# Block 2's gate in seven half-size products, with two of four weight sums made by accumulating DMAs

## The chip, the cores and the metric

One NeuronCore of a Trainium2 chip runs the whole kernel in one launch. The metric is the device time in microseconds (us); the median of three runs of the kernel before is 755.2 us. The engines spoken of are TensorE (PE, with its weight loads PEld), VectorE (DVE), ScalarE (ACT), GpSimd (POOL) and SyncE (SP), whose queue issues all DMAs of the kernel before.

## The reference, cut to what matters

One layer of a streaming encoder on x of shape (1, 256, 1024) in float32: a feed-forward, a mixer (attention and a spatial gate), a second feed-forward. The change touches the two feed-forwards:

```python
D_MODEL, D_FF, SEQ = 1024, 4096, 256
def swiglu(h, w_gate, w_up, w_down):
    return (jax.nn.silu(h @ w_gate) * (h @ w_up)) @ w_down
...
h = rmsnorm(x, ffn1_pre_g[l])
x = x + 0.5 * rmsnorm(swiglu(h, ffn1_w_gate[l], ffn1_w_up[l], ffn1_w_down[l]), ffn1_post_g[l])
...                                   # mixer
h = rmsnorm(x, ffn2_pre_g[l])
x = x + 0.5 * rmsnorm(swiglu(h, ffn2_w_gate[l], ffn2_w_up[l], ffn2_w_down[l]), ffn2_post_g[l])
```

## The kernel before

Every float32 operand of a matmul is split in two parts of a narrower type, hi and lo, and a product is made of three matmuls (hi by hi, hi by lo, lo by hi). `split` (L84) does it: ACT casts the raw data to hi (L85), DVE subtracts to get lo (L86). Weights come from HBM in tiles of 128 x 2048 float32 (1 MB). `load` (L97) takes a buffer of the pool `raws` (5 buffers) and issues the DMA on SP's queue (L101); `parts_of` (L104) takes a pair of the pool `wts` (4 buffers each of hi and lo) and splits into it.

A feed-forward, `ffn` (L346), goes over four blocks of 1024 of the 4096 hidden columns. In each block it makes gate, then up, then multiplies them (L375), transposes the result on PE (hp, L383) and keeps it, split, as hT. The down projection of a block's eight slices (`down`, L352, matmuls L362 into y) is not done in the block but handed out between the steps of the next block: with 8 slices and `total` steps in a block, slice number 8·at/total is done after step `at`. Two slices share one 1 MB tile of down weights.

The product of a block is 256 rows x 1024 inputs by 1024 x 1024 weights. It is made in one of two ways:

- `section` (L225): eight steps of 12 matmuls of 128 x 512; a step is half a weight tile for both row halves. Four weight tiles are loaded and split.
- `fast` (L282): Strassen's scheme in Winograd's form on the 2 x 2 halves of rows, inputs and columns: seven products of 12 matmuls (L297) instead of eight. The sums of the activations come from `sums` (L264), once for each feed-forward. The sums of weight tiles b11, b12, b21, b22 are four DVE additions of 128 x 2048 (`add`, L301): b11+b12 for product p5, then +b22 for p6, b12+b22 for p7, and the p6 sum +b21 for p4; they are made in place in the raw tiles. Five DVE additions of 128 x 512 (`mixed`, L305) put the products together, and one ACT copy (L312) keeps p1. The order of the steps is p1, p5, p6, p2, p7, p3, p4. Seven tiles are split.

FAST1 and FAST2 say which products go the fast way: up in blocks 1, 2 and 3 of each feed-forward. Gate goes by sections everywhere. The mixer uses sections alone (FASTM is empty).

The Tile framework sets the order of work on each engine when the kernel is built: an instruction takes its place in its engine's queue by its place in the program, as soon as its operands and its buffer are there in the framework's own reckoning, so work of later steps is taken ahead as far as buffers allow. On the chip each queue then runs in that order.

Of the kernel before, what the change touches and what calls it, by code (L numbers as in the profile page):

```python
# [18 lines left out]
ALU = mybir.AluOpType  # L19
# [15 lines left out]
NB = 4  # L35
# [1 line left out]
HOLD = 2  # L37
WARM = 14
FORGET, SCORES, TURN = 5, 3, 3
FAST1 = {(b, "u") for b in range(1, NB)}  # L40
FAST2 = {(b, "u") for b in range(1, NB)}
FASTM = set()


# [1 line left out]
def block(ctx: ExitStack, tc: tile.TileContext, a: dict, out: bass.AP):  # L46
    nc = tc.nc
# [11 lines left out]
    def bank(name):  # L59
        return psum.tile([P, 512], F32, tag="ps", name=name)  # L60
# [164 lines left out]
    def section(src, name, done, first=None, within=None):  # L225

        for c in range(2):
            pss = [bank(f"{name}{t}{c}") for t in range(NT)]  # L230
            for kh in range(2):
                early = first and (c, kh) == (0, 0)
                w = first[kh] if first and c == 0 else quarter(src[c, kh], f"{name}{c}{kh}")
                for i in range(2):
                    if early:
                        for j in range(2):
                            if (i, j) == (1, 1):
                                within()
                            proj(pss[i], i, w, kh, j, 2)
                    else:  # L240
                        for t in range(NT):
                            proj(pss[t], t, w, kh, i, 2)
                    if kh == 1 and i == 1:
                        for t in range(NT):
                            done(t, c, pss[t])
                    yield
# [32 lines left out]
            split(parts[:, i, :, 0, :], parts[:, i, :, 1, :], v[i].rearrange("p (k c) -> p k c", c=P))  # L279
        return parts  # L280

    def fast(src, name, parts, done):  # L282
        def get(c, kh):
            return load(src[c, kh], f"{name}{c}{kh}")

        def lhs_x(kh, t):
            return lambda k, xs: xT[:, kh * 4 + k, t, xs, :]

        def lhs_s(i):
            return lambda k, xs: parts[0][:, i, k, xs, :]  # L290

        def product(ps, lhs, raw, nm, start):
            w = parts_of(raw, f"{name}{nm}")
            for k in range(4):
                hi, lo = [z[:, k * 512:(k + 1) * 512] for z in w]
                for q, (xs, z) in enumerate(((0, hi), (0, lo), (1, hi))):
                    nc.tensor.matmul(ps, lhsT=lhs(k, xs), rhs=z, start=start and k == 0 and q == 0,  # L297
                                     stop=k == 3 and q == 2, skip_group_check=True)

        def add(out, p, q):  # L300
            nc.vector.tensor_tensor(out=out, in0=p, in1=q, op=ALU.add)  # L301

        def mixed(nm, p, q, op):
            o = mid_tile([P, 512], f"{name}{nm}")
            nc.vector.tensor_tensor(out=o, in0=p, in1=q, op=op)  # L305
            return o

        b11 = get(0, 0)
        a = bank(f"{name}A")
        product(a, lhs_x(0, 0), b11, "p1", True)  # L310
        p1 = mid_tile([P, 512], f"{name}p1")
        nc.scalar.copy(out=p1, in_=a)  # L312
        yield
        b12 = get(1, 0)
        add(b11, b11, b12)
        c = bank(f"{name}C")
        product(c, lhs_s(0), b11, "p5", True)
        yield
        b22 = get(1, 1)
        add(b11, b11, b22)  # L320
        b = bank(f"{name}B")
        product(b, lhs_s(1), b11, "p6", True)
        u2 = mixed("u2", b, p1, ALU.add)
        w = mixed("w", c, u2, ALU.subtract)
        yield
        add(b12, b12, b22)
        b21 = get(0, 1)
        product(a, lhs_x(1, 0), b21, "p2", False)
        done(0, 0, a)
        yield  # L330
        d = bank(f"{name}D")
        product(d, lhs_s(2), b12, "p7", True)
        done(1, 1, mixed("y11", w, d, ALU.subtract))
        yield
        product(c, lhs_s(3), b22, "p3", False)
        done(0, 1, mixed("y01", c, u2, ALU.subtract))
        yield
        add(b11, b11, b21)
        product(d, lhs_x(1, 1), b11, "p4", False)
        done(1, 0, mixed("y10", d, u2, ALU.add))  # L340
        yield
# [4 lines left out]
    def ffn(n, quick, done, before=None, after=None, first=None, within=None):  # L346


        gs, us, dn = a[f"g{n}"], a[f"u{n}"], a[f"dn{n}"]
        hTs, ys, downs, sgs = {}, {}, {}, {}  # L350

        def down(f, t, cs=(0, 1)):  # L352
            if f not in downs:
                w = quarter(dn[f // 2], f"d{n}_{f}")
                for i in range(2):
                    downs[f + i] = [v[:, i * 1024:(i + 1) * 1024] for v in w]
            if t not in ys:
                ys[t] = [bank(f"y{n}_{t}{c}") for c in range(2)]
            hi, lo = downs[f]
            for q, (xs, w) in enumerate(((0, hi), (0, lo), (1, hi))):  # L360
                for c in cs:
                    nc.tensor.matmul(ys[t][c], lhsT=hTs[f // 4][:, f % 4, t, xs, :], rhs=w[:, c * 512:(c + 1) * 512],  # L362
                                     start=f == 0 and q == 0, stop=f == NF - 1 and q == 2)

        def gate_done(b):
            def go(t, c, y):
                sg = mid_tile([P, 512], f"sg{n}_{b}{t}{c}")
                nc.scalar.activation(out=sg, in_=y, func=AF.Silu)  # L368
                sgs[t, c] = sg
            return go  # L370

        def up_done(b):
            def go(t, c, y):
                h = sgs[t, c]
                nc.vector.tensor_tensor(out=h, in0=y, in1=h, op=ALU.mult)  # L375

                def turn():
                    f4 = 2 * b + c
                    if f4 not in hTs:
                        hTs[f4] = big.tile([P, 4, NT, 2, P], F32R, tag="b", name=f"hT{n}_{f4}")  # L380
                    ps = bank(f"hp{n}_{b}{t}{c}")
                    for i in range(4):
                        nc.tensor.transpose(out=ps[:, i * P:(i + 1) * P], in_=h[:, i * P:(i + 1) * P], identity=ident)  # L383
                    marks[n, f4] = split(hTs[f4][:, :, t, 0, :], hTs[f4][:, :, t, 1, :],
                                         ps.rearrange("p (i c) -> p i c", c=P))[1]
                later(2, turn)
            return go

        side, parts = [], []
        for b in range(NB):  # L390
            steps = []
            for src, kind, fn in ((gs[b], "g", gate_done(b)), (us[b], "u", up_done(b))):
                nm = f"{kind}{n}_{b}"
                if (b, kind) == (0, "g"):
                    steps.append((section(src, nm, fn, first, within) if first else section_by_tile(src, nm, fn, 4), 8))
                elif (b, kind) in quick:
                    steps.append((fast(src, nm, parts, fn), 7))
                else:
                    steps.append((section(src, nm, fn), 8))
            total = sum(k for _, k in steps)  # L400
            keep = HOLD if b == NB - 1 else 0
            had, gone, at = len(side) - keep, 0, 0
            for gen, _ in steps:
                for _ in gen:
                    at += 1
                    if b == 0 and at == 4 and before:
                        before()
                    if b == 0 and at == 9 and quick:
                        parts.append(sums(f"f{n}"))
                    tick()  # L410
                    while had > 0 and gone < had * at // total:
                        f = side.pop(0)
                        down(f, 0)
                        down(f, 1)
                        gone += 1
            side += range(8 * b, 8 * b + 8)
        for f in side[:HOLD]:
            down(f, 0)
            down(f, 1)
            tick()  # L420
        late = side[HOLD:]
        for f in late:
            down(f, 0)
        done(0, ys[0])
        for f in late[:-KEEP]:
            down(f, 1)
        if after:
            after()
        for c in range(2):
            for f in late[-KEEP:]:  # L430
                down(f, 1, (c,))
        done(1, ys[1])


    def run(gen):
        for _ in gen:
            tick()
# [113 lines left out]
    def mixer(turn_in):  # L551
# [8 lines left out]
        parts = [sums("mx")] if FASTM else None  # L560

        def columns(src, name, done):
            run(fast(src, name, parts, done) if name in FASTM else section(src, name, done))

        oA = attention(v, *kept)

# [213 lines left out]
```

## Time and profile of the kernel before

| | |
|---|---|
| median of 3 runs | 755.2 us (754.33 to 756.26) |
| profiled execution, its own time | 755.46 us |
| its span from first to last instruction | 753.7 us |
| PE busy | 739.6 us, 98% of the span |
| DVE busy | 544.5 us, 72% |
| ACT busy | 380.0 us, 50% |
| POOL busy | 12.9 us, 2% |
| granted TensorE clock, mean | 0.993 of full speed |
| DMA | 141.62 MB, mean 188 GB/s, all on SP's queue but for instruction fetches |

The page gives busy time by engine; the timeline gives instructions with their start, duration, and the idle time of the engine before them with what ended it. A matmul's shown duration overlaps the next one's, so the pace of PE is read from starts, not durations. "PEld" is the weight load that runs beside matmuls.

### The profile page before, as it was taken

How to read it: one execution, taken by the hardware profiler on the slowest of the kernel's cores; microseconds unless marked ns; L12 is line 12 of the kernel's file. 1: busy time of each engine (PE TensorE's matmuls, PEld its weight loads, DVE VectorE, ACT ScalarE, POOL GpSimd, SP SyncE). 2: the span in 40 equal slices, each digit the busy share in tenths (PEclk: the TensorE clock that was granted, in tenths of full speed). 3: DMA queues.
4: the chain of work that ended last, by engine and by line, in shares of the span. 5: the costliest groups of instructions: out<-in, count | busy, mean ns of one | idle time of the engine just before them, and what ended most of it. 6: DMA issues, size and time to landing. Idle time of an engine off the chain costs nothing.

```text
span 753.7 us, 8526 instructions
## 1 busy us (share of the span) xinstructions
PE 739.6 (98%) x3446; PEld 608.8 (81%) x3446; DVE 544.5 (72%) x565; ACT 380.0 (50%) x397; POOL 12.9 (2%) x20
## 2 busy tenths in 40 slices
PE   7999999999999999999999999999999999999996
PEld 4888888888888877888888888878888888888885
DVE  5964798689479886745487547878489868947973
ACT  3853465456445464754544435755346535634541
POOL 0000000000000010000010000100000000000000
PEclk8999999999999999999999999999999999999999
DMA  9876168428515835743336435357416832841611
GB/s 331 327 265 230 57 227 301 142 80 340 195 57 212 328 147 187 264 168 113 129 149 262 154 143 223 136 176 275 168 56 237 306 126 93 343 178 57 223 56 57
DMA packets 22695, 141.62 MB, mean 188 GB/s; under 512 B 3264, under 2 KB 3520, under 8 KB 6528
## 3 DMA queue, kind: packets, MB, share of 16 engines
q1 hardware_dynamic: 22656, 141.08, 51.2%
q8 instruction: 27, 0.44, 0.2%
q14 instruction: 12, 0.10, 0.1%
HBM read 140.02 MB, written 1.05 MB: 187 GB/s over the span
## 4 chain that ended last, share of the span: by engine, by line
PE 91%; DVE 4%; issue 1%; POOL 1%; ACT 1%; DMA 1%; SPq 0%; POOLq 0%; DVEq 0%; ACTq 0%
PE g L222 22%; PE y L362 22%; PE u L222 9%; PE qk L201 4%; PE sv L222 3%; PE ga L222 3%; PE gb L222 3%; PE qk L202 2%; PE hp L383 2%; PE v L222 2%; PE u_3D L297 1%; PE u_1C L297 1%; PE u_1D L297 1%; PE u_2C L297 1%; PE wo L222 1%; PE u_2D L297 1%
## 5 line engine op out<-in xcount | busy, mean ns | idle before, releaser
L222 PE MATMUL g<-hi_g,xT 128*128 128x512 f32 x512 | 166.1, 395 | 0.5 <-ACT xT L85 0.5
L362 PE MATMUL y<-hi_d,hT 128*128 128x512 f32 x512 | 147.0, 391 | 0.0
L222 PEld LDWEIGHTS g<-hi_g,xT 128*128 128x128 f32 x512 | 97.2, 190 | 21.4 <-ACT xT L85 1.3
L362 PEld LDWEIGHTS y<-hi_d,hT 128*128 128x128 f32 x512 | 95.7, 188 | 19.4
L86 DVE TENSOR_TENSOR lo_g<-raw_g,hi_g 128x2048 fp32r<-128x2048 f32 (+1 forms) x50 | 75.0, 1520 | 42.0 <-ACT hi_g L85 42.0
L222 PE MATMUL g<-lo_g,xT 128*128 128x512 f32 x256 | 100.7, 393 | 1.1 <-DVE lo_g L86 1.1
L86 DVE TENSOR_TENSOR lo_d<-raw_d,hi_d 128x2048 fp32r<-128x2048 f32 x32 | 73.1, 2289 | 36.7 <-ACT hi_d L85 36.5
L362 PE MATMUL y<-lo_d,hT 128*128 128x512 f32 x256 | 80.5, 392 | 0.0
L85 ACT CAST hi_g<-raw_g 128x2048 fp32r<-128x2048 f32 (+1 forms) x50 | 62.8, 1292 | 32.8 <-PE u L222 9.3
L85 ACT CAST hi_d<-raw_d 128x2048 fp32r<-128x2048 f32 x32 | 60.8, 1913 | 25.4 <-PE g L222 8.6
L222 PE MATMUL u<-hi_u,xT 128*128 128x512 f32 x192 | 60.6, 391 | 0.0
L222 PEld LDWEIGHTS g<-lo_g,xT 128*128 128x128 f32 x256 | 48.6, 190 | 12.0 <-DVE lo_g L86 2.2
L362 PEld LDWEIGHTS y<-lo_d,hT 128*128 128x128 f32 x256 | 47.9, 188 | 9.7
L301 DVE TENSOR_TENSOR raw_u<-raw_u,raw_u 128x2048 f32<-128x2048 f32 x24 | 55.0, 2292 | 0.8
L368 ACT ACTIVATE sg<-g 128x512 f32<-128x512 f32 x32 | 18.8, 598 | 60.5 <-PE g L222 60.5
L201 PE MATMUL qk<-xT,hi_qk 128*128 128x512 f32 x128 | 46.3, 403 | 0.0
L85 ACT CAST hi_u_3p<-raw_u 128x2048 fp32r<-128x2048 f32 x14 | 26.6, 1916 | 32.9 <-DVE raw_u L301 26.0
L222 PEld LDWEIGHTS u<-hi_u,xT 128*128 128x128 f32 x192 | 36.1, 188 | 7.3
L86 DVE TENSOR_TENSOR lo_u_3p<-raw_u,hi_u_3p 128x2048 fp32r<-128x2048 f32 x14 | 31.9, 2289 | 9.4 <-ACT hi_u_3p L85 9.4
L222 PE MATMUL u<-lo_u,xT 128*128 128x512 f32 x96 | 37.4, 389 | 0.0
L85 ACT CAST hi_u_2p<-raw_u 128x2048 fp32r<-128x2048 f32 x14 | 26.9, 1918 | 20.1 <-DVE raw_u L301 9.5
L85 ACT CAST hi_u_1p<-raw_u 128x2048 fp32r<-128x2048 f32 x14 | 26.8, 1917 | 20.1 <-DVE raw_u L301 9.5
(256 smaller groups left out, 1267.1 us busy)
## 6 DMA issues: line engine op xcount, KB each, us to landing
raw_u<-in_u SPq DMA_DIRECT2D x32, 1024.0 KB, 4.8
raw_d<-in_dn SPq DMA_DIRECT2D x32, 1024.0 KB, 4.8
raw_g<-in_g SPq DMA_DIRECT2D x30, 1024.0 KB, 4.8
raw_qk<-in_w_qk SPq DMA_DIRECT2D x8, 1024.0 KB, 5.2
raw_v<-in_w_v SPq DMA_DIRECT2D x4, 1024.0 KB, 5.2
raw_sv<-in_w_sv SPq DMA_DIRECT2D x4, 1024.0 KB, 4.7
raw_u<-in_w_u SPq DMA_DIRECT2D x4, 1024.0 KB, 4.7
raw_ga<-in_w_ga SPq DMA_DIRECT2D x4, 1024.0 KB, 4.8
```

The lines of the kernel that those rows point to most:

```text
L85: return [nc.scalar.copy(out=hi, in_=src), nc.vector.tensor_tensor(out=lo, in0=src, in1=hi.bitcast(F32), op=ALU.subtract)]
L86: nc.vector.tensor_tensor(out=lo, in0=src, in1=hi.bitcast(F32), op=ALU.subtract)]
L201: nc.tensor.matmul(ps, lhsT=hi, rhs=xT[:, k], start=k == 0, stop=False, skip_group_check=True)
L202: nc.tensor.matmul(top, lhsT=lo, rhs=xT[:, k, :, 0, :], start=False, stop=k == KT - 1, skip_group_check=True)
L222: nc.tensor.matmul(ps, lhsT=xT[:, kh * 4 + k, t, xs, :], rhs=v, start=kh == 0 and k == 0 and q == 0, stop=kh == 1 and k == 3 and q == 2)
L297: nc.tensor.matmul(ps, lhsT=lhs(k, xs), rhs=z, start=start and k == 0 and q == 0, stop=k == 3 and q == 2, skip_group_check=True)
L301: nc.vector.tensor_tensor(out=out, in0=p, in1=q, op=ALU.add)
L362: nc.tensor.matmul(ys[t][c], lhsT=hTs[f // 4][:, f % 4, t, xs, :], rhs=w[:, c * 512:(c + 1) * 512], start=f == 0 and q == 0, stop=f == NF ...
L368: nc.scalar.activation(out=sg, in_=y, func=AF.Silu)
L383: nc.tensor.transpose(out=ps[:, i * P:(i + 1) * P], in_=h[:, i * P:(i + 1) * P], identity=ident)
```

## The change

In both feed-forwards the gate of block 2 goes through `fast` too. `fast` has a new argument, `dma`, which is true for gate and up of block 2 and false for up of blocks 1 and 3. Where it is true, two of the four weight sums are not made on DVE: `two` loads one tile with SP's queue into a raw buffer, and then POOL's queue issues a second DMA of the same size that adds another weight tile from HBM to that buffer (`accum_op`). It is used for b12+b11 (p5) and b12+b22 (p7). b11 and b22 are loaded as tiles of their own as well, b12 no longer is.

```diff
-FAST1 = {(b, "u") for b in range(1, NB)}
-FAST2 = {(b, "u") for b in range(1, NB)}
+FAST1 = {(b, "u") for b in range(1, NB)} | {(2, "g")}
+FAST2 = FAST1
...
-    def fast(src, name, parts, done):
+    def fast(src, name, parts, done, dma):
...
+        def two(first, second):
+
+            raw = get(*first)
+            nc.gpsimd.dma_start(out=raw, in_=src[second], accum_op=ALU.add)
+            return raw
...
-        b12 = get(1, 0)
-        add(b11, b11, b12)
+        if dma:
+            t1 = two((1, 0), (0, 0))
+        else:
+            b12 = get(1, 0)
+            add(b11, b11, b12)
+            t1 = b11
         c = bank(f"{name}C")
-        product(c, lhs_s(0), b11, "p5", True)
+        product(c, lhs_s(0), t1, "p5", True)
         yield
         b22 = get(1, 1)
-        add(b11, b11, b22)
+        add(b11, t1, b22)
...
-        add(b12, b12, b22)
         b21 = get(0, 1)
         product(a, lhs_x(1, 0), b21, "p2", False)
...
+        if not dma:
+            add(b12, b12, b22)
         d = bank(f"{name}D")
-        product(d, lhs_s(2), b12, "p7", True)
+        product(d, lhs_s(2), two((1, 0), (1, 1)) if dma else b12, "p7", True)
...
-                    steps.append((fast(src, nm, parts, fn), 7))
+                    steps.append((fast(src, nm, parts, fn, (b, "g") in quick), 7))
```

For up of blocks 1 and 3 the one difference is that b12+b22 is written one step later in the program (after p2 in place of before it).

## Rows read from the trace of the kernel before

**Rows 1.** The page, its first part: busy time, share of span, instructions.
```profile
span 753.7 us, 8526 instructions
PE 739.6 (98%) x3446; PEld 608.8 (81%) x3446; DVE 544.5 (72%) x565; ACT 380.0 (50%) x397; POOL 12.9 (2%) x20
```
**Rows 2.** Busy time in block 2 of the feed-forwards; last columns: clock, DMA share, GB/s.
```profile
core 0: us, PE busy (x) PEld busy (x) DVE busy (x) ACT busy (x) POOL busy (x), PEclk, DMA share, GB/s
124.72:189.20 64.48, 64.48 (x294) 53.27 (x292) 50.89 (x33) 33.53 (x24) 0.00 (x0) 1.00 0.53 195
595.12:659.58 64.46, 64.46 (x293) 53.26 (x292) 50.89 (x33) 33.52 (x24) 0.00 (x0) 1.00 0.53 196
```
**Rows 3.** Timeline of PE in block 2: start, duration, engine, line, operation, tiles.
```profile
124.72 0.39 PE L222 MATMUL g<-hi_g,xT 128*128 128x512 f32 x1
...
157.85 0.39 PE L297 MATMUL u_2A<-hi_u_2p,xT 128*128 128x512 f32 x1
...
160.57 0.39 PE L297 MATMUL u_2C<-hi_u_2p,parts_f 128*128 128x512 f32 x1
...
163.29 0.62 PE L362 MATMUL y<-hi_d,hT 128*128 128x512 f32 x2
...
166.01 0.39 PE L297 MATMUL u_2B<-hi_u_2p,parts_f 128*128 128x512 f32 x1
...
176.90 0.60 PE L383 MATMUL hp<-ident,sg 128*128 128x128 f32 x4
177.25 0.48 PE L297 MATMUL u_2C<-hi_u_2p,parts_f 128*128 128x512 f32 x1
```
**Rows 4.** Groups by line: count, busy us, mean ns, idle before and its releaser.
```profile
L85 ACT CAST hi_u_2p<-raw_u 128x2048 fp32r<-128x2048 f32 x14 | 26.9, 1918 | 20.1 <-DVE raw_u L301 9.5 <-PE u_2B L297 6.9 <-PE y L362 2.9
L86 DVE TENSOR_TENSOR lo_u_2p<-raw_u,hi_u_2p 128x2048 fp32r<-128x2048 f32 x14 | 31.9, 2290 | 1.7 <-ACT hi_u_2p L85 1.7
L301 DVE TENSOR_TENSOR raw_u<-raw_u,raw_u 128x2048 f32<-128x2048 f32 x24 | 55.0, 2292 | 0.8
```
**Rows 5.** Timeline of DVE in block 2's up: starts of large and small instructions.
```profile
176.32 2.29 DVE L86 TENSOR_TENSOR lo_u_2p<-raw_u,hi_u_2p 128x2048 fp32r<-128x2048 f32 x1 [0.35 <-ACT hi_u_2p L85]
178.53 0.68 DVE L305 TENSOR_TENSOR u_2y<-u_2w,u_2D 128x512 f32<-128x512 f32 x1
179.13 2.29 DVE L86 TENSOR_TENSOR lo_g<-raw_g,hi_g 128x2048 fp32r<-128x2048 f32 x1
```
**Rows 6.** Timeline of ACT there: a cast follows the product that frees its buffer.
```profile
174.37 1.92 ACT L85 CAST hi_u_2p<-raw_u 128x2048 fp32r<-128x2048 f32 x1 [0.80 <-PE y L362]
```
**Rows 7.** Timeline of SP's queue: weight loads issued for block 2 (first feed-forward).
```profile
102.34 0.33 SPq L101 DMA_DIRECT2D raw_g<-in_g  x1
104.54 0.33 SPq L101 DMA_DIRECT2D raw_d<-in_dn  x1
108.69 3.13 SPq L101 DMA_DIRECT2D raw_g<-in_g  x2
114.13 0.33 SPq L101 DMA_DIRECT2D raw_d<-in_dn  x1
116.93 0.33 SPq L101 DMA_DIRECT2D raw_g<-in_g  x1
120.93 5.38 SPq L101 DMA_DIRECT2D raw_u<-in_u  x2
```
**Rows 8.** DMA view of 95 to 132: GB/s in 40 slices, then kinds of queues.
```profile
GB/s 0 71 221 443 399 0 0 0 35 159 390 425 425 425 354 124 151 425 425 239 407 425 354 425 425 283 434 416 71 159 399 425 151 0 71 230 425 407 142 425
q1 hardware_dynamic: 1360, 9.96, 72.3%
```
**Rows 9.** The page, DMA issues: KB each, median us from issue to landing.
```profile
raw_u<-in_u SPq DMA_DIRECT2D x32, 1024.0 KB, 4.8
raw_g<-in_g SPq DMA_DIRECT2D x30, 1024.0 KB, 4.8
```
**Rows 10.** Timeline of DVE around the start of block 2 (PE starts it at 124.72).
```profile
114.61 2.28 DVE L86 TENSOR_TENSOR lo_g<-raw_g,hi_g 128x2048 fp32r<-128x2048 f32 x1
...
118.61 2.28 DVE L86 TENSOR_TENSOR lo_d<-raw_d,hi_d 128x2048 fp32r<-128x2048 f32 x1
...
132.80 2.29 DVE L86 TENSOR_TENSOR lo_d<-raw_d,hi_d 128x2048 fp32r<-128x2048 f32 x1 [3.04 <-ACT hi_d L85]
141.44 2.29 DVE L86 TENSOR_TENSOR lo_g<-raw_g,hi_g 128x2048 fp32r<-128x2048 f32 x1 [6.35 <-ACT hi_g L85]
```

More of the change, by code (lines that the diff above doesn't have):

```diff
@@ L562, in columns @@
         def columns(src, name, done):
-            run(fast(src, name, parts, done) if name in FASTM else section(src, name, done))
+            run(fast(src, name, parts, done, True) if name in FASTM else section(src, name, done))
         oA = attention(v, *kept)
```

## The prediction, made before the changed kernel was run

> **What bounds the kernel now.** I read the busy times first, then block 2 of both feed-forwards as a stretch of its own, then its timelines engine by engine. PE is busy for 739.6 of 753.7 us [rows 1], and in block 2 for all of its 64.48 and 64.46 us, at the full clock [rows 2]; nothing there ends a wait of PE. So a matmul taken out of block 2 shortens the kernel, as long as nothing else becomes late. DVE is next: 50.9 us busy in the same stretches, 79%; ACT 33.5 us; the DMA engines have a share of 0.53; POOL does nothing [rows 2]. The reader should see that the margin of DVE is 13.6 us for a block, and that it isn't spread evenly: around the entry to block 2 DVE has one instruction after another and then stands idle for 3.04 and 6.35 us [rows 10].
>
> **What the change takes from PE.** Starts of the first matmuls give the pace: p1 of up at 157.85, p5 at 160.57, the down slice behind it at 163.29, p6 at 166.01: 2.72 us for 12 matmuls [rows 3]. Gate has eight such steps by sections and seven by `fast`. One step less in each feed-forward is 2 x 2.72 = 5.44 us. The profiled execution took 755.46 us, 0.26 above the median of the runs; 755.46 - 5.44 = **750.0 us** if nothing turns late. The matmuls that stay have the same shape, so I take their pace as unchanged.
>
> **What it adds to ACT.** Gate splits seven tiles for four, 3 x 1.92 us [rows 4], and copies p1. Block 2 goes from 33.5 to some 40 us of 61.8: hidden by PE's work, costs nothing unless a cast stands in line behind one that waits (below).
>
> **What it adds to DVE.** After the change block 2 has 14 weight subtractions for gate and up, 4 for the down tiles, and 4 weight additions (two a product), all of 128 x 2048 and 2.29 us [rows 4]; and 10 of `mixed`, 4 of gate times up and 4 of hT, all of 0.68. Back to back the large ones start 2.21 us and the small ones 0.60 us apart [rows 5], so 22 x 2.21 + 18 x 0.60 = 59.4 us, for a block that PE now does in 64.48 - 2.72 = 61.76 us. That is 96%. With all four sums on DVE it would be 26 x 2.21 + 10.8 = 68.3 us, more than PE has: the two sums by DMA are what makes room at all. At the entry I added up what DVE must do from 114.61 [rows 10] before p6 of gate, with PE starting p1 at 124.72, p5 at 127.8 and p6 at 133.6 (products, one down slice, two transposes of 0.35 from [rows 3]): subtractions for p1, the first down tile, p5, the sum and the subtraction for p6 and nine small ones left by block 1: 5 x 2.21 + 9 x 0.60 = 16.5, done at 131.1. Margin 2.5 us; behind p6 it grows to 5. So DVE alone costs nothing in the sum, and up to 2.5 us of its waits are covered.
>
> **What it adds to DMA.** Block 2 loads 14 tiles and adds 4 by DMA, where it loaded 12. The engines move up to 425 GB/s [rows 8], 2.47 us for 1 MB; an addition has to read the tile in the buffer as well, so 2.47 to 4.94 us. Together 44 to 54 us of 61.8: not a bound, but bursts will meet.
>
> **The unknown: how long an accumulating DMA takes** (A, from the end of the load to the sum landed). The trace has no DMA from POOL and none that adds; all its data go by SP's hardware queue [rows 8]. Nearest row: a plain 1 MB load, 4.8 us from issue to landing [rows 9], of which 2.47 is data. Below that it can't be, as it moves at least the same bytes. Two streams of data behind the same 2.3 us of latency make 7.2; two plain loads one after the other, 9.6, which I take as the upper bound. Other loads run at the same time in this stretch (354 to 425 GB/s in many slices [rows 8]), so I take **8**. Nothing else waits in POOL's queue in block 2 [rows 2], so POOL waiting for the load costs nobody else anything. SP's queue isn't held by it either: it only issues one load the more.
>
> **Where A meets a deadline.** A raw buffer that gets a sum is held for 4.8 + A, then needs a cast and a subtraction, 176.32 + 2.29 - 174.37 = 4.24 us from the start of the cast [rows 5, 6]. With five raw buffers, of which b11 is held from p1 to p4 and b22 from p6 to p3, the question is when a buffer comes free. Times are of the first feed-forward.
> - p5 of gate: second load slot at 104.54 [rows 7], landed 109.3, due as cast at 127.8 - 4.24 = 123.6: room for A = 14. No stall.
> - p7 of gate: the buffer of the first down tile comes free after its subtraction (118.61 + 2.28), and the load goes at 120.93 as one does today [rows 7, 10]; landed 125.7; p7 is due at 141.7: room for A = 11.7.
> - p5 of up: PE would start it at 158.05. The five buffers then hold gate's b11, b21, b22, its p7 sum and a down tile. The first to come free goes to up's b11, the next to this sum: when p3 of gate is split. Its pair of `wts` comes free with the end of p6 (136.3), and cast, subtraction and DVE's queue of then (two `mixed`, p7's subtraction) bring that to 140.5 to 142. Load landed 145.3 to 146.8, to be cast by 153.8: room for A = 7.0 to 8.5. **This is the place where it is tight.**
> - p7 of up: the next buffer is that of a down tile, free at 153 to 157, landed 158 to 162, due at 171.65: room for A = 5.6 to 9.4.
>
> With A = 8 and the late buffer, p5 of up is 1.0 us late, and p7 of up moves with it. I charge 1.0 us in each feed-forward: 750.0 + 2.0 = **752.0 us**. In block 3 all is as before, DVE has room there, and up of blocks 1 and 3 keeps its additions.
>
> **Rivals.**
> 1. *The gain is eaten by the late sums.* A = 9.6 and the late buffers: p5 of up 2.6 us late, p7 of up (9.6 - 5.6) = 4.0 us. 5.2 to 8.0 us in both feed-forwards, 755.2 to 758: no change, or a little slower. For it: five buffers, four of them held long. Against it: the framework can take the down tile's split ahead of a sum that hasn't landed, which frees its buffer at 153.
> 2. *DVE becomes the bound.* It is planned at 96% of PE's time; a loss of 5% of its time to waits for other engines makes 59.4 / 0.95 = 62.5, 0.8 us over in each feed-forward: 750.0 + 1.6 = 751.6, and more if a subtraction that waits for a late sum stands in front of others in its queue. It is near my forecast, and I count it there.
> 3. *Slower: the sums come much later than two plain loads.* One mechanism: an in-order queue (ACT's cast, then DVE's subtraction) waits on a sum at its head, with the other weights' casts and hT behind it, so what the sum lacks PE loses. It starts from POOL: it writes the descriptors itself, while DVE works without a break. If each addition waits for two DVE instructions of 2.29 and takes 8 + 4.6, about 12.6, then p5 of up is 5.6 us late and p7 of up 7.0: 11 to 14 us in all, 761 to 764. It decides from 3.9 us a feed-forward on (5.44 + 2.27 over two), that is A above about 9.5 to 11. For it: DVE busy 59.4 of 61.8 us. Against it: no row shows POOL and DVE in each other's way, since POOL hardly works.
>
> The Trainium skill has a rule that speaks against the change, in "SBUF — State Buffer", section "Summary: rules for kernel authors": a DMA issued from GpSimd under VectorE work starves in its descriptor generation while VectorE is in its fast modes; issue it elsewhere. The same page, section "Who interferes with whom", says that `tensor_tensor` has no such two-port mode. The rows speak for the second: DVE takes 2.29 us for 2048 columns [rows 4], under one column a nanosecond. So rival 3 keeps a chance, but not the main one.
>
> That the change doesn't do what it says would need the framework to keep PE waiting on something else, such as a bank of PSUM: gate needs four of the eight (y holds four), up's p1 takes over gate's bank after p2. I see no case there.
>
> **How the numbers follow.** About 0.3% is what a measurement of this kernel can tell from no change: 2.27 us, so faster is under 752.9, slower over 757.5. Forecast (stalls up to 1.4 us a feed-forward, rival 2 in it): 0.52. Rival 1 with its low end: 0.28, of which 0.24 fall within 0.3% and 0.04 above. Rival 3: 0.20. Faster 0.52, same 0.24, slower 0.24. The range starts at 749.3, which is 750.0 with the spread of the runs, and goes to 759: it takes in A from 4.8 to 9.6 and leaves out most of rival 3.
>
> **What would show it.** Right: matmuls down by 24; block 2 of 61.8 to 63 us; the only new idle time of PE ahead of p5 or p7 of up, released by DVE or ACT behind a DMA; DVE over 90% busy in block 2; DMAs on a POOL queue landing 7 to 9 us after their issue. Rival 1: idle time of 2.6 us and more there. Rival 3: sums landing after 12 us and more, gaps at p5 of gate too. Wrong altogether: idle PE in blocks 1 or 3, a lower clock, or a longer end of the kernel behind the last matmul.

## The result, and the profile after

The changed kernel takes 792.15 us (median of five runs, 789.78 to 800.66) where the kernel before takes 755.2: 1.051 times as long [1.046, 1.056]. 752.0 was predicted. The profiled execution took 791.31 us with a span of 789.2, so that 35.5 us of span are to be explained [rows 1].

The page of the changed kernel: span, busy times, shares of the chain that ended last, and the new DMA issues on POOL's queue (KB each, median us from issue to landing).

```profile
span 789.2 us, 8546 instructions
PE 747.0 (95%) x3422; PEld 611.2 (77%) x3422; DVE 562.5 (71%) x581; ACT 389.5 (49%) x405; POOL 20.1 (3%) x28
...
PE 67%; DMA 15%; DVE 11%; ACT 3%; issue 2%; POOL 1%; SPq 0%; POOLq 0%; DVEq 0%; ACTq 0%
...
raw_u<-in_u POOLq DMA_DIRECT2D x4, 1024.0 KB, 11.1
...
raw_g<-in_g POOLq DMA_DIRECT2D x4, 1024.0 KB, 9.0
```

PE has the 24 matmuls less that were planned (3446 to 3422), and yet is busy 7.4 us longer: some of them ran slower. DMA holds 15% of the chain that ended last.

Where the time went is read from PE's timeline (start, duration, then in brackets the idle time before and its releaser), block 2 of the first feed-forward:

```profile
121.45 0.39 PE L374 MATMUL y<-hi_d,hT 128*128 128x512 f32 x1
128.87 1.09 PE L395 MATMUL hp<-ident,sg 128*128 128x128 f32 x4 [7.03 <-DVE sg L387]
...
170.99 0.80 PE L298 MATMUL u_2C<-hi_u_2p,parts_f 128*128 128x512 f32 x1 [4.39 <-ACT hi_u_2p L85]
174.16 0.80 PE L298 MATMUL u_2C<-lo_u_2p,parts_f 128*128 128x512 f32 x1 [2.38 <-DVE lo_u_2p L86]
192.61 0.50 PE L298 MATMUL u_2D<-lo_u_2p,parts_f 128*128 128x512 f32 x1 [1.83 <-DVE lo_u_2p L86]
```

Four waits of PE: one at the entry to the block, two at p5 of up (bank u_2C), one at p7 of up (u_2D). Set against the starts of [rows 3], stage by stage (starts of first matmuls, us):

| stage, first feed-forward | before | after | lengthened by | of it idle |
|---|---|---|---|---|
| start of block 2's gate | 124.72 | 133.32 | 8.60 | 7.03 |
| gate, to p1 of up | 33.13 | 30.40 | -2.73 | 0 |
| p1 and p5 of up, to p6 | 8.16 | 18.44 | 10.28 | 6.77 |
| p6 of up, to p7 | 8.16 | 8.16 | 0 | 0 |
| p7 of up, to gate of block 3 | 15.03 | 18.84 | 3.81 | 1.83 |
| sum | | | 19.96 | 15.63 |

Gate gives back its 2.72 us as planned. The three late places cost 22.7 us, 15.6 of them idle. Some 6.0 of the other 7.1 are work at a lower clock: from the first matmul after the wait to the end of the stage PE took 1.49, 2.79 and 1.75 us longer than the kernel before for the same matmuls. The second feed-forward shows the same places (3.60, 4.68, 2.38 and 1.2 us idle, and 0.6 more for sg), and its block 3 starts 35.9 us later than before.

The clock is seen in the busy times by stretch (columns as in [rows 2]):

```profile
core 0: us, PE busy (x) PEld busy (x) DVE busy (x) ACT busy (x) POOL busy (x), PEclk, DMA share, GB/s
124.50:206.00 81.50, 68.54 (x280) 55.18 (x281) 60.78 (x42) 40.25 (x30) 2.62 (x3) 0.87 0.69 219
128.00:132.00 4.00, 3.13 (x10) 2.68 (x11) 4.00 (x5) 0.67 (x2) 0.00 (x0) 0.50 0.00 0
172.00:176.00 4.00, 1.84 (x4) 1.49 (x5) 4.00 (x2) 4.00 (x5) 0.00 (x0) 0.50 0.21 37
110.90:123.80 12.90, 10.94 (x53) 8.65 (x51) 7.41 (x7) 3.24 (x3) 1.00 (x1) 1.00 0.98 300
```

Where [rows 2] have a granted clock of 1.00 throughout, here it is 0.87, and 0.50 (1.2 of 2.4 GHz) for some us after PE had stood idle. The last row, the time of the first adding DMA, is for later: the DMA engines are full, at 300 GB/s.

Two more views say why PE waited at the entry. ACT's timeline, and then DVE's:

```profile
114.37 0.58 ACT L85 CAST hT<-hp 128x512 fp32r<-128x512 f32 x1
123.90 1.90 ACT L85 CAST hi_g_2p<-raw_g 128x2048 fp32r<-128x2048 f32 x1 [8.95 <-DMA raw_g<-in_g]
125.71 0.58 ACT L85 CAST hT<-hp 128x512 fp32r<-128x512 f32 x1
```
```profile
125.83 2.29 DVE L86 TENSOR_TENSOR lo_g_2p<-raw_g,hi_g_2p 128x2048 fp32r<-128x2048 f32 x1 [7.17 <-ACT hi_g_2p L85]
128.04 0.68 DVE L387 TENSOR_TENSOR sg<-u_1y,sg 128x512 f32<-128x512 f32 x1
...
169.01 2.29 DVE L302 TENSOR_TENSOR raw_u<-raw_u,raw_u 128x2048 f32<-128x2048 f32 x1 [9.12 <-DMA raw_u<-in_u]
171.22 0.68 DVE L306 TENSOR_TENSOR g_2y<-g_2D,g_2u 128x512 f32<-128x512 f32 x1
171.82 2.28 DVE L86 TENSOR_TENSOR lo_u_2p<-raw_u,hi_u_2p 128x2048 fp32r<-128x2048 f32 x1
```

The cast of gate's p5 sum stands in ACT's queue in front of the second of block 1's four hT casts. It waits 8.95 us for the sum, and behind it wait that hT and, on DVE behind the subtraction, sg, which PE wants at 121.8 for the third of block 1's four groups of transposes (121.76 in the kernel before). Neither has anything to do with the sum; the wait of PE is for sg. At p5 of up DVE has p6's addition, which reads the same sum, at the head of its queue, and p5's own subtraction comes third: that is PE's second wait there, 2.38 us.

The chain that ended last (start us, duration us, what) has the sums themselves: a load, then its addition (the load of the second addition, 132.18 to 136.99, is not on this chain):

```profile
104.51 5.63 DMA raw_g<-in_g
...
110.88 12.92 DMA raw_g<-in_g
...
137.56 7.99 DMA raw_g<-in_g
...
149.91 4.78 DMA raw_u<-in_u
...
155.25 13.68 DMA raw_u<-in_u
...
174.13 4.94 DMA raw_u<-in_u
...
179.63 8.59 DMA raw_u<-in_u
```

A load takes 4.8 to 5.6 us, POOL starts the addition 0.5 to 0.75 us after it has landed, and the addition takes 12.9, 8.0, 13.7, 8.6 us here and 9.9, 8.1, 14.1, 8.3 in the second feed-forward: mean 10.4. The A of the prediction has POOL's start in it as well: 11.0 on average, where 8 was taken and 9.6 was the upper bound.

### The profile page after: what moved, and what is told of

It reads as the page before. It is cut to its first block, busy times and chain, and to the rows that moved or that the text cites. A ratio compares the mean times of both kernels' runs of the same rounds, so it can differ in the third digit from the quotient of the medians.

```text
span 789.2 us, 8546 instructions
## 1 busy us (share of the span) xinstructions
PE 747.0 (95%) x3422; PEld 611.2 (77%) x3422; DVE 562.5 (71%) x581; ACT 389.5 (49%) x405; POOL 20.1 (3%) x28
## 3 DMA queue, kind: packets, MB, share of 16 engines
HBM read 152.60 MB, written 1.05 MB: 195 GB/s over the span
## 4 chain that ended last, share of the span: by engine, by line
PE 67%; DMA 15%; DVE 11%; ACT 3%; issue 2%; POOL 1%; SPq 0%; POOLq 0%; DVEq 0%; ACTq 0%
PE g L222 16%; PE y L374 14%; PE u L222 8%; DMA raw_u<-in_u 8%; DMA raw_g<-in_g 6%; PE qk L201 4%; PE sv L222 3%; PE ga L222 3%; PE gb L222 3%; PE qk L202 2%; DVE lo_u_1p L86 2%; PE v L222 2%; PE hp L395 2%; DVE lo_u_2p L86 1%; PE u_3D L298 1%
## 5 line engine op out<-in xcount | busy, mean ns | idle before, releaser
L374 PE MATMUL y<-hi_d,hT 128*128 128x512 f32 x512 | 149.2, 397 | 0.0
L222 PE MATMUL g<-hi_g,xT 128*128 128x512 f32 x384 | 124.3, 395 | 0.5 <-ACT xT L85 0.5
L222 PEld LDWEIGHTS g<-hi_g,xT 128*128 128x128 f32 x384 | 73.0, 190 | 16.3 <-ACT xT L85 1.3
L222 PE MATMUL g<-lo_g,xT 128*128 128x512 f32 x192 | 75.7, 394 | 1.1 <-DVE lo_g L86 1.1
L86 DVE TENSOR_TENSOR lo_g<-raw_g,hi_g 128x512 fp32r<-128x512 f32 (+1 forms) x42 | 56.6, 1371 | 24.9 <-ACT hi_g L85 24.9
L302 DVE TENSOR_TENSOR raw_u<-raw_u,raw_u 128x2048 f32<-128x2048 f32 x20 | 45.8, 2290 | 19.1 <-DMA raw_u<-in_u 18.6
L85 ACT CAST hi_g<-raw_g 128x512 fp32r<-128x512 f32 (+1 forms) x42 | 47.5, 1175 | 23.6 <-PE u L222 9.3
L374 PEld LDWEIGHTS y<-lo_d,hT 128*128 128x128 f32 x256 | 48.8, 192 | 10.1
L85 ACT CAST hi_g_2p<-raw_g 128x2048 fp32r<-128x2048 f32 x14 | 26.6, 1913 | 35.6 <-DMA raw_g<-in_g 27.5
L222 PEld LDWEIGHTS g<-lo_g,xT 128*128 128x128 f32 x192 | 36.5, 190 | 9.5 <-DVE lo_g L86 2.2
L86 DVE TENSOR_TENSOR lo_g_2p<-raw_g,hi_g_2p 128x2048 fp32r<-128x2048 f32 x14 | 31.9, 2289 | 15.2 <-ACT hi_g_2p L85 15.1
## 6 DMA issues: line engine op xcount, KB each, us to landing
raw_u<-in_u POOLq DMA_DIRECT2D x4, 1024.0 KB, 11.1
```

The lines of the kernel that those rows point to most:

```text
L85: return [nc.scalar.copy(out=hi, in_=src), nc.vector.tensor_tensor(out=lo, in0=src, in1=hi.bitcast(F32), op=ALU.subtract)]
L86: nc.vector.tensor_tensor(out=lo, in0=src, in1=hi.bitcast(F32), op=ALU.subtract)]
L222: nc.tensor.matmul(ps, lhsT=xT[:, kh * 4 + k, t, xs, :], rhs=v, start=kh == 0 and k == 0 and q == 0, stop=kh == 1 and k == 3 and q == 2)
```

## The experiments

Ratios are to the kernel before, from runs on the same chip (755.1 us, within 0.4). Line numbers in the rows are those of the kernel that each comes from. Three theories were to be told apart: the sums come late (how long they take, or when they are asked for); an in-order queue hands the lateness to work that doesn't need it; DVE is short of time, or POOL is kept waiting by DVE.

**All four sums on DVE, gate fast.** No DMA adds anything.

```diff
-steps.append((fast(src, nm, parts, fn, (b, "g") in quick), 7))
+steps.append((fast(src, nm, parts, fn, False), 7))
```

> Gate of block 2 in seven products, but all four weight sums of gate and of up on VectorE; no DMA that adds. Late sums (the 37 us come from sums that land 8 to 14 us after their load, with casts and other work waiting behind them): the losses of the changed kernel go; what stays is VectorE, 26 x 2.21 + 18 x 0.60 = 68.3 us of work in block 2 for 61.8 of TensorE, so 4 to 6.5 us late in each feed-forward: 758 to 763 us. Seven products for gate are bad in themselves (PSUM banks, middle tiles, order of the queues): 785 us and more.

770.86 us, 1.021 [1.019, 1.023], above the 758 to 763 expected. Block 2, busy times, and DVE's two longest waits in it (us in total, times, longest):

```profile
124.70:194.90 70.20, 63.85 (x270) 50.49 (x269) 62.12 (x42) 35.82 (x28) 0.00 (x0) 0.95 0.45 165
```
```profile
DVE lo_g_2p L86 <- ACT hi_g_2p L85: 3.4, 2, 2.0
DVE lo_u_2p L86 <- ACT hi_u_2p L85: 2.9, 2, 2.0
```

The block takes 70.2 us, near the 68.3 that were worked out for DVE with all four sums, but not by way of a full DVE, so the nearness is luck: DVE is busy for 62.1 us, with 42 of the 44 instructions in the stretch, and idle for 8.1. In 6.3 of these it waits for ACT's casts, and the casts in turn wait for DVE's additions (17.1 us in all); the clock falls there too. So the fast gate with its sums on DVE costs 15.8 us. That comes with 62.1 us of work for DVE in a block that PE could do in 61.8, and waits between DVE and ACT; which of them costs how much is not shown. The changed kernel is another 21 us slower.

**Only up's sums by DMA, gate by sections.**

```diff
-FAST1 = {(b, "u") for b in range(1, NB)} | {(2, "g")}
+FAST1 = {(b, "u") for b in range(1, NB)}
-... fast(src, nm, parts, fn, (b, "g") in quick)
+... fast(src, nm, parts, fn, b == 2)
```

> Gate of block 2 by sections as in the kernel before, up of block 2 with two of its sums by adding DMAs. TensorE's work is that of the kernel before, VectorE has 4.4 us a block less. Late sums: the load for p5 can go some 25 us before p5 is due (b12 is loaded at 126 for 160.6 in the kernel before), the sum lands in time, but its cast may hold the casts behind it: 755 to 765 us. If adding DMAs cost by what they do to other transfers or engines while they run, wherever the sum is due: 770 us and more (half of the 37 us).

754.64 us, 1.000 [0.999, 1.001], and PE waits for nothing in block 2. POOL's timeline has the first of its four additions; then two stretches of 1 us within the second addition, and one of the kernel before in which plain loads run:

```profile
131.49 1.02 POOL L312 DMA_DIRECT2D raw_u<-in_u  x1 [121.69 <-DMA raw_u<-in_u]
```
```profile
160.00:161.00 1.00, 1.00 (x6) 0.84 (x5) 1.00 (x2) 0.20 (x2) 0.00 (x0) 1.00 1.03 213
162.00:163.00 1.00, 1.00 (x6) 0.84 (x5) 0.97 (x2) 1.00 (x1) 0.00 (x0) 1.00 1.02 213
```
```profile
117.00:118.00 1.00, 1.00 (x9) 0.77 (x7) 1.00 (x2) 0.71 (x1) 0.00 (x0) 1.00 0.99 418
```

In the two stretches no other DMA runs: an addition by itself fills the DMA engines (share 1.02 to 1.03) and moves 213 GB/s, half of the 418 of plain loads. The four additions take 8.4 to 8.6 us, with 0.5 to 1.3 MB of SP's loads in the same time. Here p5's was asked for at 131.5 for a product due at 160.6, and so it harms nobody; and DVE is 97 to 100% busy in the two stretches without making this addition longer than the others.

**The second DMA plain, on SP's queue.** It overwrites instead of adding, so the two sums are left out of the computation.

```diff
-nc.gpsimd.dma_start(out=raw, in_=src[second], accum_op=ALU.add)
+nc.sync.dma_start(out=raw, in_=src[second])
```

> The changed kernel with a plain second load from SP's queue in place of the adding DMA, into the same buffer, after the first: p5 and p7 of block 2 use b11 and b22 in place of the sums b12+b11 and b12+b22, the additions of b12 are left out. Same buffers, same order of loads from HBM, same work of TensorE, ACT and VectorE. Late sums: the second load lands 4.8 us behind the first and all of the loss goes: 750 to 754 us. VectorE's shortage, or HBM traffic of two more megabytes a product: 775 us and more stay.

753.16 us, 0.998 [0.996, 0.999], within the 750 to 754 expected; the second loads took 5.1 to 7.5 us, and PE waited 0.9, 0.8 and 0.5 us in block 2 of the first feed-forward. The order of work on PE, DVE and ACT isn't quite that of the changed kernel here.

**The second DMA plain, on POOL's queue.** The two sums are left out as well; ACT and DVE have the same instructions in the same order as in the changed kernel.

```diff
-nc.gpsimd.dma_start(out=raw, in_=src[second], accum_op=ALU.add)
+nc.gpsimd.dma_start(out=raw, in_=src[second])
```

> As the run with the second load from SP's queue, but issued from POOL's queue and still plain: p5 and p7 of block 2 use b11 and b22 in place of the sums; only the addition is left out of the DMA. If the addition (the second read and the adder) makes the sum late: it lands 5 to 7 us behind the first load, 750 to 758 us. If POOL's software queue makes it late, beside SP's loads: it lands after 10 us and more, 775 to 795 us.

763.33 us, 1.010 [1.006, 1.014], which is neither of the two ranges. From the chain that ended last, the four second DMAs:

```profile
110.16 7.61 DMA raw_g<-in_g
...
131.42 5.49 DMA raw_g<-in_g
...
146.62 10.08 DMA raw_u<-in_u
...
167.18 5.04 DMA raw_u<-in_u
```

With order and queues as in the changed kernel, 28.8 of its 36.9 us go when the DMA doesn't add. PE still waits 1.68 us for sg at the entry and 2.57 us at p5 of up. Even the plain second load takes 7.6 and 10.1 us in the two places where the addition took 12.9 and 13.7, and 5.5 and 5.0 us where that took 8.0 and 8.6. The two kernels with a plain second load are 10.2 us apart; the queue that issues it is one difference, the order of the engines' work another, so how much the issue from POOL's queue costs is not shown.

**Gate's p5 cast behind the third hT cast.** The order is set by hand; all else is as in the changed kernel.

```diff
+if nm == "p5" and name[0] == "g":
+    in_order([turned[-2], made[0][0]])
```

> The changed kernel with one order added: in ACT's queue the cast of gate's p5 sum stands behind the third hT cast of block 1 in place of ahead of the second. Head of the queue (the sum of gate's p5 isn't late for TensorE, its waiting cast holds hT): the 8.6 us at the entry to block 2 go to 1 or less in each feed-forward, and the losses at p5 and p7 of up (9.9 and 3.7) stay: 774 to 780 us. If the sum itself is late for p5 of gate, moving the cast back helps nothing: 788 us and more.

796.51 us, 1.054 [1.050, 1.057]: no gain at all, and my theory that ACT's queue at the entry was a cost by itself fell. DVE's timeline at the entry, and PE's four longest waits in the first feed-forward (us in total, times, longest):

```profile
122.47 2.29 DVE L306 TENSOR_TENSOR raw_g<-raw_g,raw_g 128x2048 f32<-128x2048 f32 x1 [3.87 <-DMA raw_g<-in_g]
124.68 0.68 DVE L395 TENSOR_TENSOR sg<-u_1y,sg 128x512 f32<-128x512 f32 x1
```
```profile
PE u_2C L302 <- ACT hi_u_2p L86: 4.0, 2, 3.1
PE hp L403 <- DVE sg L395: 3.7, 1, 3.7
PE u_2D L302 <- ACT hi_u_2p L86: 2.8, 1, 2.8
PE g_2D L302 <- DVE lo_g_2p L87: 1.8, 1, 1.8
```

The wait went from ACT to DVE, where p6's addition of the same sum stands in front of sg. The entry cost 5.3 us in place of 8.6 (gate starts at 130.0), and the 3.3 us saved came back at p7 of gate, which had not waited before, and at p7 of up (2.8 in place of 1.83): block 3 starts at 209.6 in place of 209.2.

**One sum by DMA at a time.** `two` for p7 alone, p5 on DVE; then for p5 alone, p7 on DVE with its own load of b12.

```diff
-if dma:
+if "p5" in dma:
     t1 = two((1, 0), (0, 0))
...
-product(d, lhs_s(2), two((1, 0), (1, 1)) if dma else b12, "p7", True)
+product(d, lhs_s(2), two((1, 0), (1, 1)) if "p7" in dma else b12, "p7", True)
```

p7 alone:

> Gate and up of block 2 in seven products, the sum for p7 by the adding DMA, that for p5 on VectorE. Late sums: p5's losses (8.6 at the entry, 9.9 at p5 of up) go; VectorE has 24 large instructions, 63.8 us for 61.8, some 2 us late, p7 of up 0 to 4: 754 to 762 us. If two adding DMAs in a feed-forward cost what four cost by half: 772 us.

p5 alone:

> The other half: the sum for p5 by the adding DMA, that for p7 on VectorE from a load of b12 of its own. Late sums: the losses at the entry and at p5 of up stay, that of p7 of up goes, VectorE loses some 2 us: 785 to 790 us. Cost shared by half: 772 us.

p7 alone: 764.66 us, 1.013 [1.012, 1.015], higher than expected: DVE has three sums to make for gate and three for up, is busy 61.3 us, and block 2 takes 68.9. p5 alone: 781.09 us, 1.035 [1.033, 1.036], under the 785 to 790 expected, with additions of 11.0 and 14.0 us. PE's waits of it:

```profile
PE hp L399 <- DVE sg L391: 9.8, 2, 4.9
PE u_2C L299 <- ACT hi_u_2p L86: 6.5, 2, 3.4
PE u_2C L299 <- DVE lo_u_2p L87: 4.2, 2, 2.1
```

So p5's sums are the more harmful ones: without them 27.5 of the 36.9 us go, without p7's 11.1. With p7's alone the waits of PE in block 2 come to 8.1 us in both feed-forwards, all of them at p5 of up and for sg, where no sum by DMA is due; with p5's alone 20.5 us of waits stand at the two places seen before. Both kernels also lack DVE time, so the costs of the two sums can't be added up to the change's.

**Gate's sums by DMA with the cast order of above, up's p5 on DVE, its p7 by DMA.**

```diff
+SUMS = {(2, "g"): ("p5", "p7"), (2, "u"): ("p7",)}
...
+    in_order([turned[-2], made[0][0]])
```

> Gate with both sums by adding DMAs and the cast of p5 behind the third hT cast, up with the sum for p5 on VectorE and that for p7 by DMA: every sum has room for 11 us and more but that of up's p7. VectorE 23 large instructions, 61.6 of 61.8 us. Late sums: 751 to 758 us, the low end is faster than both kernels. If an adding DMA slows other work while it runs, wherever it stands: 770 us and more.

776.19 us, 1.028 [1.026, 1.030], a miss of 18 us and more; by its number it is in the range of the other theory of this run, that an adding DMA slows other work wherever it stands. But the trace has the late sum again: gate's first addition took 12.3 us, PE waited 13.0 us for sg in all, and p7 of gate was late too. The next four kernels change when a sum is asked for.

**Six raw buffers, and asking early.** A sixth raw buffer needs room, which the pool `mid` gives (10 buffers to 6); one kernel shrinks `mid` alone. "Early" means that both `two` stand at the start of `fast`, p5's ahead of b11's load, p7's right behind it.

```diff
-raws = ctx.enter_context(tc.tile_pool(name="raws", bufs=5))
+raws = ctx.enter_context(tc.tile_pool(name="raws", bufs=6))
-mid = ctx.enter_context(tc.tile_pool(name="mid", bufs=10))
+mid = ctx.enter_context(tc.tile_pool(name="mid", bufs=6))
...
+if dma:
+    t1 = two((1, 0), (0, 0))
 b11 = get(0, 0)
+if dma:
+    t7 = two((1, 0), (1, 1))
...
-product(d, lhs_s(2), two((1, 0), (1, 1)) if dma else b12, "p7", True)
+product(d, lhs_s(2), t7 if dma else b12, "p7", True)
```

Six buffers, asked for late:

> The changed kernel with six raw buffers for five; to make room the pool of middle tiles has 6 for 10. Buffer loop (each sum holds a buffer for load, wait and add, so the loop of five buffers sets the pace of block 2, and a wait taken away at one place comes back at the next): one more buffer lets up's loads go 8 us earlier; the losses at p5 and p7 of up (9.9 and 3.7 us) go to 0 to 3, the entry keeps what comes from the head of the queues: 762 to 772 us. Head of the queues alone: 785 us and more.

Five buffers and the smaller `mid`, asked for late:

> Control for the six buffers: the changed kernel with five raw buffers and only the pool of middle tiles cut from 10 to 6. All theories: as the changed kernel, 788 to 797 us; more would say that the middle tiles cost something.

Six buffers, asked for early:

> Six raw buffers, and both sums of a product asked for at its start in the program (p5's before b11, p7's behind b11), so that their buffers come first. Buffer loop: all sums land before they are due but perhaps gate's p5: 751 to 762 us. Company of loads (the adding DMA takes 13 us beside others wherever it stands) with the queues' heads: 770 us and more.

Five buffers (`mid` at 10), asked for early:

> The changed kernel with five raw buffers and ten middle tiles as it has them, and only the order of asking changed: p5's sum before b11, p7's behind b11. Separates the order from the sixth buffer. If the early asking is what counts (a sum's chain of load, wait and add starts one or two buffers earlier, the plain loads of b22 and b21 need little time and can come later): 750 to 758 us. If the sixth buffer is what counts: 770 to 790 us, with TensorE waiting at p6 or p2 for plain tiles or at p5 of up.

| median us, ratio | asked for as in the change | asked for early |
|---|---|---|
| five raw buffers | 792.15, 1.051; with `mid` of 6: 790.26, 1.049 [1.045, 1.052] | 768.63, 1.019 [1.015, 1.022] |
| six raw buffers | 764.64, 1.013 [1.011, 1.015] | 750.21, 0.994 [0.992, 0.996] |

Six buffers asked for late, and the control with the smaller `mid`, came out in their ranges; six asked for early is a little under its range. Five asked for early is in neither of its two: both the order and the buffer count. Each of the two takes off 23.5 or 27.5 us by itself, both together 42; `mid` has no part in it. The last kernel is the quickest of all, 5 us under the kernel before, and its block 2 is what the prediction planned. Busy times of that block, POOL's first addition, the cast of gate's p5 sum on ACT, and PE's longest wait between 90 and 700 us:

```profile
124.70:186.40 61.70, 61.70 (x281) 51.04 (x280) 59.52 (x42) 39.44 (x28) 1.75 (x2) 1.00 0.89 309
```
```profile
101.06 1.02 POOL L312 DMA_DIRECT2D raw_g<-in_g  x1 [91.06 <-DMA raw_g<-in_g]
```
```profile
115.76 1.92 ACT L85 CAST hi_g_2p<-raw_g 128x2048 fp32r<-128x2048 f32 x1 [0.80 <-PE u_1C L298]
```
```profile
PE g L222 <- DVE lo_g L86: 1.1, 1, 1.1
```

That wait, for a split of gate's weights by sections, is not in block 2 of either feed-forward. The additions are no shorter: 9.0 to 13.3 us, mean 10.9 (the changed kernel's: 10.4). They only start earlier, the first at 101.1 in place of 110.9 (106.5 and 106.9 in the two kernels between). The cast of gate's p5 sum stands in ACT's queue where it stands in the changed kernel, ahead of the second hT cast, and p5's subtraction stands ahead of the same sg on DVE; but the sum has landed by then, at 110.3, and the cast waits for PE and not for a DMA. So it is the time of the sum, and not another order of the queues, that took away the wait at the entry. With five buffers the early kernel still waits:

```profile
PE y L376 <- DVE lo_d L86: 5.7, 1, 5.7
PE hp L397 <- DVE sg L389: 2.7, 2, 2.2
PE u_2A L298 <- DVE lo_u_2p L86: 2.1, 1, 2.1
```

A down tile and p1 of up, products that have no sum, are late there, and sg at the entry, behind a sum that still lands too late (at 118.1). The first two fit sums that hold two of the five buffers for longer, so that plain loads have to wait for one; six buffers in the same order have no such waits.

## Why the prediction was wrong, step by step

**What PE saves: right.** 24 matmuls fewer, gate 2.73 us shorter, and the floor of 750.0 us is where the kernel with early sums and six buffers stands (750.05 in its profile).

**ACT and DVE: right as sums.** ACT is busy 39.4 us in that block (40 said), DVE 59.52 of 61.70 us (59.4 of 61.76), and PE doesn't wait. So 96% is enough if the sums are there in time. With all four sums on DVE block 2 takes 70.2 us where 68.3 were said, but DVE is idle for 8.1 of them.

**The length of an addition: right beside few loads, wrong beside many.** 8 us was taken, and the changed kernel has four additions of 8.0 to 8.6 us, the up-alone kernel four of 8.4 to 8.6. The upper bound, 9.6 from two plain loads in a row, was no bound: the loads that SP has in flight, which spoke for 8 in the prediction, have no part in it. What SP's queue moved while the first and the second addition of the changed kernel ran (packets, MB, share of the engines):

```profile
q1 hardware_dynamic: 383, 2.81, 58.0%
```
```profile
q1 hardware_dynamic: 144, 1.05, 33.7%
```

Beside 2.81 MB the addition took 12.92 us, beside 1.05 MB 7.99. In the first 3.9 us of the longer one POOL's queue moved no data, and SP's 1.27 MB. In all profiles of the kernels here the additions with up to 1.3 MB of loads in the same time took 7.8 to 9.6 us, those with 2.5 MB and more 11.9 to 14.2. (A longer addition also has time for more loads, so this goes with the reading and doesn't prove it.) Plain second loads on POOL's queue are stretched at the same two places (7.6 and 10.1 us, 5.0 and 5.5 elsewhere).

**"p5 of gate: room for A = 14, no stall": the step that failed first.** The load landed at 110.1 (109.3 said), and the cast could start at 123.9, when 123.6 was the time reckoned for it: PE's own need of that product was met but for 0.3 us. The stall of 7.03 us came from what stands behind the cast, and so behind its subtraction in DVE's queue: sg of block 1, which PE needed at 121.8. The deadline was taken from the product that uses the sum, and not from the work behind it in the queues. Nothing was charged for the entry; it cost 8.60 us in the first feed-forward. The order by hand shows that ACT's queue is not alone in this: p6's addition does the same on DVE.

**p5 of up: right place, wrong size.** Its load landed at 154.69; less the 8.6 us by which the block began late that is 146.1, within the 145.3 to 146.8 of the prediction. For that landing the room was 7.7 us; A was 14.2, 0.56 for POOL's start and 13.68 for the addition, so the sum came 6.5 us too late, and PE's idle time there is 6.77. 1.0 us was charged; with the clock the place cost 10.28. The term that was mis-sized is A: 8 taken, 14.2 measured. p7 of up behaves likewise: load landed at 179.07, less the 18.9 us of delay by then 160.2 (158 to 162 said), and 1.83 us idle; nothing was charged for it, and it cost 3.81.

**The clock: left out.** "A lower clock" was named as what would make the prediction wrong altogether, and no term of the sum had it. It cost some 6.0 of 22.7 us in the first feed-forward: at each of the three late places some us of work ran at half the clock.

**Rival 3: right in its mechanism and sign, wrong in its source.** A late sum at the head of in-order queues, 12.6 us long, is what was seen, at 12.9 and 13.7. But POOL waiting for DVE is not what made it late: POOL starts each addition 0.5 to 0.75 us after the load has landed, and the instruction that issues it takes 0.86 to 1.02 us, with DVE at 96% as well. Nor are the additions longest where DVE is busiest: the first took 12.9 us with DVE busy for 7.4 of them, the second of the up-alone kernel 8.5 us with DVE busy for 7.6. The Trainium skill's rule from "SBUF — State Buffer", section "Summary: rules for kernel authors", that the descriptor generation of a GpSimd-issued DMA starves while VectorE is in its fast modes, would, if it bore on this work of DVE, have made the additions longest where DVE is busiest. The trace goes with the same page's section "Who interferes with whom", by which `tensor_copy` was seen to stall such a DMA and `tensor_tensor` was not: 8.5 us with DVE 97 to 100% busy in the stretches shown. The price worked out for the rival, 11 to 14 us, was low as well, as it had neither the entry nor the clock. A chance of 0.20 for it was too little: "For it" should have held that four sums, each of them a chain of load, POOL and addition of 13 to 20 us, were asked for in the program's order and not ahead of it.

**What settled it.** Moving the one cast gave nothing back, as the next instruction behind the late sum took its place. Taking the DMA from p5's sums gave back 27.5 us, and taking it from p7's 11.1, each with more work for DVE. Two changes that start the chains earlier, a buffer more and a request earlier, gave back all of the loss together, with the same four sums by DMA. How much of the change's cost belongs to which wait stays open for that reason. That other loads make an addition long rests on times side by side, beside few loads and beside many; no run held SP's loads back during an addition.

## What to carry to other kernels

Work that is moved from a busy engine to a chain of DMAs is judged by when the chain can start, buffer and first load included, and not by its length alone: here the same additions gave 792 us asked for late with five buffers and 750 asked for early with six. The time at which a transfer is due is that of the first instruction that stands behind its consumer in any in-order queue, not that of the product that wants it. And a wait that comes back at the next place when it is taken away at one, as with the cast that was moved here, asks for an earlier start of what is waited for: here the buffers and the request order had to change.

## What the runs showed of the hardware that was not expected

- A DMA that adds 1 MB into a buffer keeps the DMA engines full at 213 GB/s, where plain loads move 418. It took 7.8 to 9.6 us beside up to 1.3 MB of loads and 11.9 to 14.2 beside 2.5 MB and more, against 4.8 for a plain load.
- After PE had stood idle for 7.03 us, and again after 4.39 and 2.38 us, the granted clock was 0.50 (1.2 GHz) for some us of work, with matmuls starting 0.43 us apart in place of 0.227. With the stretch at p7 of up that comes to some 6.0 us beside the 15.6 us of idle time itself.
